# DeltaNet mixer: triangular inverse in eight pieces, pair assembly three tiles later, three gate tiles last

## The chip, the cores and the metric

One Trainium2 chip, one of its cores. The metric is the device time of one execution in microseconds (us), smaller is better. Shown times are medians of several runs.

## What is computed

A trunk of two layers over 512 frames of width 1024: an even layer (pooling and sparse attention), a gated DeltaNet layer, and a gated convolutional FFN after each. The change lies in the DeltaNet layer alone, whose core per head and per chunk of 64 frames is

```
proj = h @ w_in                                  # q, k, v (1024 each), gate 1024, beta 8, a 8
q, k, v = silu(causal_dwconv(qkv, conv_w))       # width 4
a     = einsum(k * beta, k) * dec_strict         # 64 x 64, strictly lower
t_mat = inverse of (a + eye)                     # triangular, unit diagonal
u, w  = t_mat @ (v * beta), t_mat @ (k * beta * exp(gc))
attn  = einsum(q, k) * dec_incl
# over the chunks:
v_new = u - w @ state;  o = q_dec @ state + attn @ v_new
state = state * decay + k_dec^T @ v_new
out   = rms_norm(o) * silu(gate) @ w_out
```

## The kernel before

Products with the large weights are made of three matmuls each (`mm3`, lines 101 to 106): weights and activations are split into a high and a low part. `split` (lines 94 to 99) makes the high part on ACT (L97) and the low part on DVE or POOL (L98, by a list). A projection tile is 128 output columns: 24 matmuls of 128x512 into one of four PSUM banks named `main`. Weights are loaded by SP (L110) three tiles ahead and split two tiles ahead.

`odd` builds the DeltaNet layer. Its loop goes over 32 projection tiles in `ORDER`: g (gate), k, q, v, each with a head number 0 to 7. After each tile it

- evacuates the tile: `gate` is one ACT instruction (L946) and a store to DRAM (L949); k, q and v tiles go through `conv`, one ACT instruction (L1020) and three of DVE (L1022), and later a SiLU on ACT (L1023);
- calls `pump`, which advances every running generator by one step. `k_chain`, `q_chain` and `v_chain` transpose and multiply a head some tiles later (L1038, L1067, L1093), and their results are read from PSUM by ACT (L1043) or DVE (L1095, L1082). POOL masks the result of L1095 (L1096). These small results use a ring of three PSUM banks named `chain`;
- writes PE's, ACT's and DVE's instructions in just this order (a manual schedule), so that each of these engines waits in order.

`invert` (lines 1100 to 1120) inverts the 32x32 diagonal blocks of all heads and chunks, on DVE alone: 31 rounds j of a product (L1114) and a subtraction (L1115), then a transposing copy (L1118), and two stores to DRAM, `x_d` (L1119) and `xt_d` (L1120). It is started at tile q3, where it only loads (L1106); a `yield` ends a piece, the next piece is issued at the next tile's `pump`. The pieces are rounds 0 to 9, 10 to 16, 17 to 23, 24 to 30, in tiles g5, q4, q5 and q6.

`y_chain` (lines 1125 to 1168) assembles the 128x128 inverses of two heads (a pair) out of these blocks. It is started four times, at the tiles in `YS`. Its steps, one a tile: load blocks from `x_d` (L1130, the first pair only) and `xt_d` (L1137) into a zeroed tile (L1132); nothing; multiply (L1143); multiply (L1150); transpose and multiply (L1158, L1160); multiply (L1167). What is not done after the last tile is done at once by `drain`. Then the recurrence over chunks of 128 frames begins: `step`, which uses the assembled inverse in L1253.

`QUIET` names the tiles whose low part is made on DVE; the other tiles' low parts of this layer are made on POOL.

Of the kernel before, what the change touches and what calls it, by code (L numbers as in the profile page):

```python
# [26 lines left out]
class Trunk:  # L27
# [89 lines left out]
    def load_rows(self, src, r0, tags=("wh", "wl"), lo_eng=None):  # L117
# [4 lines left out]

    FIRST = 5

    ORDER = [(t[0], int(t[1])) for t in ("g0 g1 g2 g3 g4 k0 k1 k2 k3 k4 k5 k6 k7 q0 q1 q2 q3 g5 "
                                         "q4 q5 q6 q7 v0 v1 v2 v3 v4 v5 v6 v7 g6 g7").split()]


    QUIET = [("q", 4), ("q", 5), ("q", 6), ("q", 7)]
    YS = [("v", 0), ("v", 2), ("v", 4), ("v", 6)]  # L130

    def tiles(self, kind):

# [2 lines left out]
        if kind == "o":  # L136
            col = {"g": 3 * D, "k": D, "q": 0, "v": 2 * D}
            return [(4 * D, 16)] + [(col[k] + n * P, P) for k, n in self.ORDER]
        return [(1152, P), (1280, P), (1408, 68), (1024, P)] + [(512 + j * P, P) for j in range(4)] + [(j * P, P) for j in (3, 2, 1, 0)]
# [760 lines left out]
    def odd(self, i, l, h):  # L900
# [5 lines left out]
        def k1(name, n=P):  # L906
            return self.s([P, n], name, bufs=1)
# [21 lines left out]
        beta, t1, t2, t3, g, gc = (k1(n, NH) for n in ("beta", "t1", "t2", "t3", "g", "gc"))  # L929
# [6 lines left out]
        v4 = lambda p: p.rearrange("p (t s) -> p t s", s=P)  # L936
# [89 lines left out]
        def silu():  # L1026

            for fn in late:
                inst = fn()
                self.after(inst, self.exp)  # L1030
                if self.hold is None:
                    self.hold = inst
            late.clear()
# [66 lines left out]
        def invert():  # L1100
            ad = a_d.rearrange("h t c s -> (h t) c s")
            As = self.b("xn", [P, 32, 32])
            Xs = self.b("xn", [P, 32, 32])
            for q in range(NB):
                r = slice(32 * q, 32 * q + 32)
                nc.sync.dma_start(As[r], ad[:, r, r])  # L1106
            nc.vector.memset(Xs, 0.0)
            nc.vector.memset(Xs.rearrange("p i j -> p (i j)")[:, ::33], 1.0)
            yield
            for j in range(31):  # L1110
                n, m = 31 - j, j + 1
                t = self.b("c", [P, 256])
                tv = t[:, :n * m].rearrange("p (i k) -> p i k", k=m)
                nc.vector.tensor_tensor(tv, As[:, j + 1:, j:j + 1].to_broadcast([P, n, m]), Xs[:, j:j + 1, :m].to_broadcast([P, n, m]), op=ALU.mult)  # L1114
                nc.vector.tensor_tensor(Xs[:, j + 1:, :m], Xs[:, j + 1:, :m], tv, op=ALU.subtract)  # L1115
                if j in (9, 16, 23):
                    yield
            nc.vector.tensor_copy(As, Xs.rearrange("p i j -> p j i"))  # L1118
            nc.sync.dma_start(x_d.rearrange("q b i j -> (q b) i j"), Xs)  # L1119
            nc.sync.dma_start(xt_d.rearrange("q b i j -> (q b) i j"), As)  # L1120
# [51 lines left out]
        nc.vector.tensor_copy(sel, self.ident[:H, :H].unsqueeze(2).to_broadcast([H, H, P]))  # L1172
        lo = [nc.gpsimd] * (len(self.ORDER) + 1)
        for kind, n in self.QUIET:
            lo[1 + self.ORDER.index((kind, n))] = nc.vector
        todo = []
        E = mybir.EngineType
        with self.tc.manual_schedule(engines={E.PE, E.Activation, E.DVE}):
            out = self.projs(win, self.tiles("o"), h, self.begin, lo)
            ba = self.b("c", [16, S])  # L1180
            nc.scalar.activation(ba, next(out), AF.Copy)
            for kind, hd in self.ORDER:
                p = next(out)
                if kind == "g":
                    silus.append(gate(hd, p))
                    if hd == 0:
                        todo = scalars(ba, silus[0])
                        next(todo)
                    elif hd == 4:
                        for _ in todo:  # L1190
                            pass
                        self.go(self.side(i))
                elif kind == "k":
                    conv(D + hd * P, p, kh(hd))
                    if hd < 3:
                        decays(range(3 * hd, min(H, 3 * hd + 3)))
                    self.go(k_chain(hd))
                elif kind == "q":
                    if hd % 2 == 0:
                        qT += pairs(1)  # L1200
                    conv(hd * P, p, qh(hd))
                    self.go(q_chain(hd))
                    if hd == 3:
                        self.go(invert())
                    if hd == 7:
                        nc.vector.scalar_tensor_tensor(c2, br2, -1.0, eg, op0=ALU.mult, op1=ALU.mult)
                else:
                    self.go(v_chain(hd, conv(2 * D + hd * P, p)))
                    if hd == 3:
                        nc.vector.tensor_scalar(fq, fq, P ** -0.5, None, op0=ALU.mult)  # L1210
                if (kind, hd) in self.YS:
                    self.go(y_chain(self.YS.index((kind, hd))))
                self.pump()
                if (kind, hd) not in self.ORDER[5:7]:
                    silu()
# [137 lines left out]
```

## Time and profile before

| | us |
|---|---|
| median of 3 runs (lowest, highest) | 1312.59 (1309.11, 1315.81) |
| the profiled execution, its own time | 1322.84 |
| its span, first to last instruction | 1320.8 |
| PE busy in the span | 1254.3 (95%) |
| DVE busy | 826.9 (63%) |
| ACT busy | 583.5 (44%) |
| POOL busy | 342.6 (26%) |

Times inside the span are counted from its first instruction. The DeltaNet projection tiles after q3 run from 742.7 to 866.6 us. Matmuls are pipelined, so the time of a row of PE is best read from one start to the next. Mean granted TensorE clock of the span: 0.969 of full speed.

### The profile page before, as it was taken

The page shows a single profiled execution, that of the slowest core. Times are in us where ns is not written, and L with a number is a line of the kernel's source. Part 1 is how long each engine was busy: PE and PEld are TensorE (multiplying, and loading weights), DVE is VectorE, ACT ScalarE, POOL GpSimd, SP SyncE. Part 2 cuts the span into 40 slices and gives each one's busy share as a digit, 9 for nine tenths or more (in the row PEclk, how much of TensorE's full clock was granted, in tenths as well). Part 3 has the DMA queues.
Part 4 walks back from the last instruction along what each step waited for, and adds up shares of the span by engine and source line. Part 5 has one row for each costly group of instructions (what it writes and reads, how often), then busy time and mean ns, then how long its engine had stood idle before and what let it go on. Part 6 is the DMA issues. An engine that isn't in the chain of part 4 may idle for free.

```text
span 1320.8 us, 17326 instructions
## 1 busy us (share of the span) xinstructions
PE 1254.3 (95%) x6359; PEld 1025.2 (78%) x6359; DVE 826.9 (63%) x1396; ACT 583.5 (44%) x1069; POOL 342.6 (26%) x294
## 2 busy tenths in 40 slices
PE   4998999899999999999999989999999999999997
PEld 3656565798888888888878868888798888888885
DVE  5599764457787678545256696436647765556328
ACT  3564656463433343326365424435655343334220
POOL 4477466350100010002356327200380010000001
PEclk9999598999999999999999999989899999999998
DMA  9952534326555538541236537473234633323221
GB/s 267 244 171 79 160 112 134 107 74 206 187 198 184 180 128 276 180 131 33 89 95 170 143 82 182 143 249 127 68 93 144 223 112 96 96 80 112 96 64 64
DMA packets 222474, 184.19 MB, mean 139 GB/s; under 512 B 24607, under 2 KB 191724, under 8 KB 222390
## 3 DMA queue, kind: packets, MB, share of 16 engines
q1 hardware_dynamic: 222390, 183.09, 45.8%
q8 instruction: 50, 0.82, 0.3%
q14 instruction: 34, 0.28, 0.1%
HBM read 169.29 MB, written 13.64 MB: 139 GB/s over the span
## 4 chain that ended last, share of the span: by engine, by line
PE 72%; DVE 12%; DMA 6%; ACT 4%; POOL 3%; issue 2%; SPq 1%; DVEq 0%; POOLq 0%; ACTq 0%
PE main L103 18%; PE main L104 18%; PE main L105 18%; PE chain L104 2%; PE chain L105 2%; PE chain L103 2%; DMA g<-in_e_mod_w_dram 1%; DVE wl L98 1%; PE side L103 1%; DVE g L716 1%; PE side L105 1%; PE side L104 1%; DVE m L715 1%; DMA mr<-in_f_mod_w_dram 1%; DVE xn L1115 1%
## 5 line engine op out<-in xcount | busy, mean ns | idle before, releaser
L103 PE MATMUL main<-h,wh 128*128 128x512 f32 (+2 forms) x1104 | 413.8, 379 | 3.6 <-ACT h L461 3.1
L104 PE MATMUL main<-h,wh 128*128 128x512 f32 (+2 forms) x1104 | 413.1, 375 | 2.7 <-DVE h L462 1.6
L105 PE MATMUL main<-h,wl 128*128 128x512 f32 (+2 forms) x1104 | 412.6, 374 | 2.3 <-DVE wl L98 1.7
L97 ACT ACTIVATE wh<-wr 128x1024 fp32r<-128x1024 f32 x176 | 184.0, 1049 | 280.6 <-PE main L104 192.9
L98 DVE TENSOR_TENSOR wl<-wr,wh 128x1024 fp32r<-128x1024 f32 x130 | 172.9, 1332 | 166.8 <-ACT wh L97 166.8
L103 PEld LDWEIGHTS main<-h,wh 128*128 128x128 f32 (+1 forms) x1104 | 207.4, 189 | 43.6 <-ACT h L461 4.1
L104 PEld LDWEIGHTS main<-h,wh 128*128 128x128 f32 (+1 forms) x1104 | 208.4, 189 | 41.2 <-DVE h L462 2.7
L105 PEld LDWEIGHTS main<-h,wl 128*128 128x128 f32 (+1 forms) x1104 | 208.1, 189 | 40.3 <-DVE wl L98 2.1
L98 POOL TENSOR_TENSOR wl<-wr,wh 128x1024 fp32r<-128x1024 f32 (+1 forms) x46 | 109.5, 2385 | 72.1 <-ACT wh L97 51.3
L542 DVE SCALAR_TENSOR_TENSOR t<-main,cw,t 128x511 f32<-128x511 f32 (+1 forms) x164 | 121.5, 744 | 2.0
L495 POOL TENSOR_TENSOR rstd<-rstd,mhalf 128x1 f32<-128x1 f32 x16 | 10.4, 651 | 395.1 <-DVE rstd L494 364.9
L1022 DVE SCALAR_TENSOR_TENSOR t<-main,ocw,t 128x511 f32<-128x511 f32 (+2 forms) x72 | 53.9, 748 | 57.5 <-ACT t L1020 55.8
L337 POOL TENSOR_TENSOR acc<-acc,mr 1x512 f32<-1x512 f32 x8 | 11.5, 1447 | 257.4 <-DVE acc L288 191.2
L282 POOL TENSOR_TENSOR acc<-acc,mr 128x512 f32<-128x512 f32 x42 | 55.2, 1321 | 33.7 <-ACT mr L280 30.7
L540 ACT ACTIVATE t<-main,cb,cw 128x512 f32<-128x512 f32 x82 | 62.2, 760 | 0.0
L547 ACT ACTIVATE t<-t 128x512 f32<-128x512 f32 x42 | 26.4, 628 | 59.5 <-DVE t L542 59.4
L103 PE MATMUL main<-wh,h 128*128 128x512 f32 x128 | 50.2, 392 | 0.0
L104 PE MATMUL main<-wl,h 128*128 128x512 f32 x128 | 50.0, 391 | 0.0
L105 PE MATMUL main<-wh,h 128*128 128x512 f32 x128 | 49.8, 390 | 0.0
L288 DVE SCALAR_TENSOR_TENSOR acc<-g,cs,acc 128x1024 f32<-128x1024 f32 x35 | 44.7, 1277 | 0.3
L280 ACT ACTIVATE mr<-mr,cs 128x512 f32<-128x512 f32 x42 | 30.1, 720 | 25.7 <-DMA mr<-in_f_mod_w_dram 12.9
L405 ACT ACTIVATE chain<-chain,B,G 128x128 f32<-128x128 f32 x84 | 33.2, 433 | 12.0 <-PE chain L397 11.4
(394 smaller groups left out, 2084.5 us busy)
## 6 DMA issues: line engine op xcount, KB each, us to landing
wr<-in_f_w_up_dram SPq DMA_DIRECT2D x84, 512.0 KB
wr<-in_f_w_down_dram SPq DMA_DIRECT2D x42, 512.0 KB
wr<-in_o_w_in_dram SPq DMA_DIRECT2D x32, 512.0 KB
g<-in_o_mod_w_dram SPq DMA_DIRECT2D x24, 512.0 KB
g<-in_e_mod_w_dram SPq DMA_DIRECT2D x32, 256.0 KB
mr<-in_f_mod_w_dram SPq DMA_DIRECT2D x32, 256.0 KB
g<-in_f_mod_w_dram SPq DMA_DIRECT2D x16, 512.0 KB
t<-in_f_mod_w_dram SPq DMA_DIRECT2D x32, 256.0 KB
```

The lines of the kernel that those rows point to most:

```text
L97: nc.scalar.activation(hi, src, AF.Copy)
L98: (lo_eng or nc.vector).tensor_tensor(lo, src, hi.bitcast(F32), op=ALU.subtract)
L103: inst = mm(ps, l[0], r[0], start=start, stop=False)
L104: mm(ps, l[0], r[1], start=False, stop=False)
L105: mm(ps, l[1], r[0], start=False, stop=stop)
L280: inst = nc.scalar.activation(r, raw, AF.Copy, scale=c)
L282: nc.gpsimd.tensor_tensor(part, part, r, op=ALU.add)
L288: nc.vector.scalar_tensor_tensor(part, raw, c, part, op0=ALU.mult, op1=ALU.add)
L405: nc.scalar.activation(t[:, c, :], t[:, c, :], AF.Identity, scale=G[:, k:k + 1], bias=B[:, k:k + 1])
L540: nc.scalar.activation(t, p, AF.Identity, bias=cb[:, n:n + 1], scale=cw[:, 4 * NF + n:4 * NF + n + 1])
L542: nc.vector.scalar_tensor_tensor(t[:, k:], p[:, :S - k], cw[:, 2 * NF * (2 - k) + n:2 * NF * (2 - k) + n + 1], t[:, k:], op0=ALU.mult, op1 ...
L1022: nc.vector.scalar_tensor_tensor(t[:, k:], p[:, :S - k], cw[:, 24 * (3 - k) + n:24 * (3 - k) + n + 1], t[:, k:], op0=ALU.mult, op1=ALU.add)
```

## The change

Three tables and one condition are altered. The gate tile g5 moves from between q3 and q4 to the end, so that the last three tiles are g5, g6, g7. `invert` yields after every fourth round, which makes eight pieces, in q4 to q7 and v0 to v3. `YS` moves the starts of the four pairs from v0, v2, v4, v6 to v3, v5, v7, g5. `QUIET` gains v0 to v3: their low parts go from POOL to DVE.

```
-    ORDER = [... "g0 g1 g2 g3 g4 k0 k1 k2 k3 k4 k5 k6 k7 q0 q1 q2 q3 g5 "
-                 "q4 q5 q6 q7 v0 v1 v2 v3 v4 v5 v6 v7 g6 g7").split()]
-    QUIET = [("q", 4), ("q", 5), ("q", 6), ("q", 7)]
-    YS = [("v", 0), ("v", 2), ("v", 4), ("v", 6)]
+    ORDER = [... "g0 g1 g2 g3 g4 k0 k1 k2 k3 k4 k5 k6 k7 q0 q1 q2 q3 q4 "
+                 "q5 q6 q7 v0 v1 v2 v3 v4 v5 v6 v7 g5 g6 g7").split()]
+    QUIET = [("q", 4), ("q", 5), ("q", 6), ("q", 7), ("v", 0), ("v", 1), ("v", 2), ("v", 3)]
+    YS = [("v", 3), ("v", 5), ("v", 7), ("g", 5)]
...
-                if j in (9, 16, 23):
+                if j % 4 == 3:
                     yield
```

How the instructions move is seen at three places. The first is SP's queue around the stores of the inverted blocks (`xn` is the blocks, `g` the tile of a pair, `wr` raw weights, `at_d` and `vb_d` results put aside for the recurrence). Before:

```order
L1119 DMA x_d<-xn_6387 128x1024
L1120 DMA xt_d<-xn_6386 128x1024
L1130 DMA xn_6812<-x_d 32x32x32 x4
L942 DMA at_d<-c_6740 128x4x128
L110 DMA wr_6906<-in_o_w_in_dram 128x8x128
L942 DMA at_d<-c_6797 128x4x128
L1137 DMA g_1258_6817<-xt_d 32x8x32 x4
```

Now:

```order
L1119 DMA x_d<-xn_6387 128x1024
L1120 DMA xt_d<-xn_6386 128x1024
L942 DMA vb_d<-c_6932 128x4x128
L110 DMA wr_7079<-in_o_w_in_dram 128x8x128
L1130 DMA xn_6935<-x_d 32x32x32 x4
L1137 DMA g_1277_6940<-xt_d 32x8x32 x4
```

The stores now end the piece in tile v3, and the loads of the first pair stand right behind them, in the same tile. Before, the stores ended the piece in q6, and the loads came in v0, two tiles later.

The second place is PE at the first matmuls on a pair's blocks (L1143). Before, they follow tile v2:

```order
L105 MATMUL main_6881<-h_834_4210,wl_6784 128x512
L1093 MATMUL chain_6917<-g_1231_6656,g_1031_5240 128x128 x4
L1038 MATMUL chain_6926<-ident,t_6787 128x128 x4
L1143 MATMUL chain_6934<-g_1258_6817,g_1036_5245 128x64 x8
L103 MATMUL main_6952<-h_831_4207,wh_6851 128x512
```

Now they follow tile v5:

```order
L105 MATMUL main_6992<-h_834_4210,wl_6906 128x512
L1038 MATMUL chain_7028<-ident,t_6909 128x128 x4
L1143 MATMUL chain_7036<-g_1277_6940,g_1036_5245 128x64 x8
L103 MATMUL main_7054<-h_831_4207,wh_6974 128x512
L104 MATMUL main_7054<-h_835_4211,wh_6974 128x512
```

From the piece that ends the inverse to L1143 there were four tiles (q7, v0, v1, v2), now there are two (v4, v5). From q3 to L1143 there were eight tiles (g5, q4 to q7, v0 to v2), now there are ten (q4 to q7, v0 to v5).

The third place is PE after the last projection tile, up to the first state update of the recurrence (L1260). Before:

```order
L105 MATMUL main_7408<-h_834_4210,wl_7285 128x512
L1167 MATMUL chain_7436<-c_7386,c_7385 64x64 x8
L1150 MATMUL chain_7446<-c_7398,xn_6812 32x32 x16
L1253 MATMUL main_7518<-h_1354_7499,g_1258_6817 128x128 x2
L1253 MATMUL main_7518<-h_1354_7499,g_1278_6945 128x128 x2
L1253 MATMUL main_7525<-h_1354_7499,g_1300_7094 128x128 x2
L1158 MATMUL chain_7466<-ident,g_1323_7252 64x64 x8
L1160 MATMUL chain_7467<-g_1323_7252,g_1039_5248 64x64 x8
L1167 MATMUL chain_7488<-c_7485,c_7484 64x64 x8
L1260 MATMUL main_7532<-c_7523,h_1355_7502 128x128 x4
```

Now:

```order
L1143 MATMUL chain_7403<-g_1327_7279,g_1039_5248 128x64 x8
L1253 MATMUL main_7518<-h_1354_7499,g_1277_6940 128x128 x2
L1253 MATMUL main_7518<-h_1354_7499,g_1294_7047 128x128 x2
L1158 MATMUL chain_7415<-ident,g_1318_7203 64x64 x8
L1160 MATMUL chain_7416<-g_1318_7203,g_1038_5247 64x64 x8
L1150 MATMUL chain_7437<-c_7412,xn_6935 32x32 x16
L1167 MATMUL chain_7456<-c_7434,c_7433 64x64 x8
L1158 MATMUL chain_7466<-ident,g_1327_7279 64x64 x8
L1160 MATMUL chain_7467<-g_1327_7279,g_1039_5248 64x64 x8
L1253 MATMUL main_7525<-h_1354_7499,g_1318_7203 128x128 x2
L1167 MATMUL chain_7488<-c_7485,c_7484 64x64 x8
L1260 MATMUL main_7532<-c_7523,h_1355_7502 128x128 x4
```

Ahead of these twelve rows stand L1167 and L1150, as before. One L1143, one L1150, one pair of L1158 and L1160 and one L1167 more than before lie behind the last tile; they lay between tiles before.

## Rows read from the trace of the kernel before

**Rows 1.** Timeline of PE after q3: start, duration, instruction, [idle before it, releaser].

```profile
742.70 0.48 PE L103 MATMUL main<-h,wh 128*128 128x512 f32 x1
...
749.51 0.48 PE L103 MATMUL main<-h,wh 128*128 128x512 f32 x1
...
762.70 0.48 PE L103 MATMUL main<-h,wh 128*128 128x512 f32 x1
...
768.59 0.48 PE L103 MATMUL main<-h,wh 128*128 128x512 f32 x1
...
770.99 0.50 PE L105 MATMUL main<-h,wl 128*128 128x512 f32 x1 [1.68 <-DVE wl L98]
...
788.60 1.11 PE L1038 MATMUL chain<-ident,g 128*128 128x128 f32 x4 [4.58 <-ACT junk L1043]
...
806.79 1.97 PE L1143 MATMUL chain<-g,g 128*128 128x64 f32 x16
```

**Rows 2.** A stretch: length, busy time of each engine, granted clock (PEclk), DMA share, GB/s.

```profile
788.60:794.60 6.00, 6.00 (x16) 4.87 (x17) 5.62 (x15) 0.00 (x0) 1.35 (x2) 0.50 0.74 249
```

**Rows 3.** Timeline of DVE, q3 to the end of the inverse.

```profile
742.37 2.32 DVE L1022 SCALAR_TENSOR_TENSOR t<-main,ocw,t 128x511 f32<-128x511 f32 x3 [1.62 <-ACT t L1020]
...
751.72 0.21 DVE L1114 TENSOR_TENSOR c<-xn,xn 128x31 f32<-128x31 f32 x1
...
758.50 1.22 DVE L98 TENSOR_TENSOR wl<-wr,wh 128x1024 fp32r<-128x1024 f32 x1
759.64 2.31 DVE L1022 SCALAR_TENSOR_TENSOR t<-main,ocw,t 128x511 f32<-128x511 f32 x3
761.86 0.68 DVE L1095 TENSOR_TENSOR c<-chain,g 128x512 f32<-128x512 f32 x1
...
762.95 1.39 DVE L1115 TENSOR_TENSOR xn<-xn,c 128x231 f32<-128x231 f32 x1
...
774.12 1.40 DVE L1115 TENSOR_TENSOR xn<-xn,c 128x252 f32<-128x252 f32 x1
775.56 2.47 DVE L1114 TENSOR_TENSOR c<-xn,xn 128x247 f32<-128x247 f32 x1
778.06 0.42 DVE L1115 TENSOR_TENSOR xn<-xn,c 128x247 f32<-128x247 f32 x1
...
786.61 2.48 DVE L1115 TENSOR_TENSOR xn<-xn,c 128x135 f32<-128x135 f32 x1
...
791.27 1.08 DVE L1118 COPY xn<-xn 128x1024 f32<-128x1024 f32 x1
```

**Rows 4.** Timeline of POOL in the same stretch.

```profile
762.62 1.46 POOL L1096 TENSOR_TENSOR c<-c,up 128x512 f32<-128x512 f32 x1 [9.91 <-DVE fq L1073]
...
775.21 2.54 POOL L98 TENSOR_TENSOR wl<-wr,wh 128x1024 fp32r<-128x1024 f32 x1
```

**Rows 5.** Timeline of SP: the issue of stores and loads (x4: four together).

```profile
738.93 0.36 SPq L1070 DMA_DIRECT2D a_d<-g  x1
741.73 2.41 SPq L1106 DMA_DIRECT2D xn<-a_d  x4
...
791.27 0.34 SPq L1119 DMA_DIRECT2D x_d<-xn  x1
...
794.62 2.20 SPq L1130 DMA_DIRECT2D xn<-x_d  x4
```

**Rows 6.** Timeline of PE after the last projection tile.

```profile
866.63 1.14 PE L1167 MATMUL chain<-c,c 64*64 64x64 f32 x16
...
868.72 1.87 PE L1253 MATMUL main<-h,g 128*128 128x128 f32 x12
870.52 0.63 PE L1158 MATMUL chain<-ident,g 64*64 64x64 f32 x8
...
872.90 1.87 PE L1167 MATMUL chain<-c,c 64*64 64x64 f32 x16 [0.68 <-ACT c L1163]
```

**Rows 7.** A stretch after the last tile, columns as in group 2.

```profile
878.00:880.00 2.00, 1.34 (x7) 1.04 (x5) 0.69 (x1) 0.63 (x2) 0.00 (x0) 0.53 0.16 66
```

More of the change, by code (lines that the diff above doesn't have):

```diff
@@ L123 @@
     FIRST = 5
-    ORDER = [(t[0], int(t[1])) for t in ("g0 g1 g2 g3 g4 k0 k1 k2 k3 k4 k5 k6 k7 q0 q1 q2 q3 g5 "
-                                         "q4 q5 q6 q7 v0 v1 v2 v3 v4 v5 v6 v7 g6 g7").split()]
-    QUIET = [("q", 4), ("q", 5), ("q", 6), ("q", 7)]
-    YS = [("v", 0), ("v", 2), ("v", 4), ("v", 6)]
+    ORDER = [(t[0], int(t[1])) for t in ("g0 g1 g2 g3 g4 k0 k1 k2 k3 k4 k5 k6 k7 q0 q1 q2 q3 q4 "
+                                         "q5 q6 q7 v0 v1 v2 v3 v4 v5 v6 v7 g5 g6 g7").split()]
+    QUIET = [("q", 4), ("q", 5), ("q", 6), ("q", 7), ("v", 0), ("v", 1), ("v", 2), ("v", 3)]
+    YS = [("v", 3), ("v", 5), ("v", 7), ("g", 5)]
     def tiles(self, kind):
```

## The prediction

> **What bounds the kernel now.** I first read the page for shares: PE is busy nearly all the time, so a change can win only where PE stands still or runs at half clock. Then the timeline of PE from q3 on, the only place that the change touches ahead of the last tiles. The reader should look at the starts there [rows 1]. A tile with its small multiplications (eight of L1093 and four transposes) takes 6.81 us from start to start (742.70 to 749.51), one with only the transposes 5.89 (762.70 to 768.59). PE's work from 742.70 to the first multiplication on a pair's blocks (L1143) would thus need 20.00 for three tiles (to 762.70), 5.89 for q6, and four times 6.81 for q7 and v0 to v2: it would be there at 795.83. It is there at 806.79. **10.96 us are lost**: 1.68 for the low part of weights that DVE makes late, 4.58 for a bank of the chain ring that ACT reads late, since ACT waits in order behind DVE [rows 1]; then 6.0 us at a granted clock of 0.50, which is 1.2 GHz [rows 2], half of which, 3.0, is lost; some 1.7 are scattered. That is 0.8% of the kernel, and all that spreading the inverse can win.
>
> The cause is DVE, whose timeline shows it without a pause from 751.72 on [rows 3]: the four pieces of the inverse stand in its order between the convolutions, the first 6.8 us long (751.72 to 758.50). The units of its work, start to start: the low part of a weight tile 1.14 (758.50 to 759.64), a convolution 2.22 (to 761.86), L1095 or L1082 0.68. From 751.72 to 791.27 are 39.55 us; two low parts, three convolutions and two L1095 take 10.30 of them. Of the 29.25 that are left, four instructions that normally take about 0.42 (as the one at 778.06) took 1.39, 1.40, 2.47 and 2.48: 6.06 too much. The inverse itself is thus 23.2 us.
>
> The timeline of POOL shows why those four were long [rows 3, 4]: POOL started the mask (L1096) at 762.62 and a low part (L98) at 775.21, and DVE's next instruction with two SBUF operands ended only when POOL had ended. So a mask beside the inverse costs 0.97, a low part on POOL beside it 2.05.
>
> **What the change removes.** The four pieces become eight, so that DVE has 23.2 us to place in eight tiles, about 2.9 in each. I count what DVE must do before the last piece ends in v3. It starts with the convolution of q4, one tile after that of q3: 742.37 + 6.81 = 749.18 [rows 1, 3]. Then come eight convolutions (17.76), five low parts (those of q7 and v0 to v3, 5.70), seven L1095 and one L1082 (5.44) and the inverse (23.2): 52.1, to 801.3. In q4, q5 and q6 the mask runs beside the piece, as at 762.62: 3 x 0.97 = 2.9. The low parts of v4 and v5 stay on POOL and start after the SiLU of v1 and v2, while their pieces run: 2 x 2.05 = 4.1. **The inverse ends at 808.3**, 17 us later than before, with DVE behind from q5 on.
>
> In q7 and v0 the mask meets a low part on DVE instead. No row shows such a meeting. It costs between 0 and 0.97 each, by the nearest rows; I take 0, since the 774.12 instruction, too, shows DVE held only for the rest of what POOL runs [rows 3], and DVE here starts about when POOL does. The Trainium skill (SBUF — State Buffer, section "SBUF: two separate sides") says that VectorE and GpSimd lock a shared port pair for a whole instruction, and that whoever starts first holds the other off. By it the two meetings are a race: lost by DVE, they would set the end 1.9 later. It also speaks against a part of this change, for a low part moved to DVE still locks the pair against POOL.
>
> **What the change adds.** The stores, then loads that wait for them, then L1143 now follow within two tiles, where there were four. The store to `x_d` was issued at 791.27 and the loads that need it at 794.62: 3.35 [rows 5]. Four loads take SP 2.20 to issue, and now eight stand in a row ahead of L1143 (L1130, L1137): 4.40. The last must land; its nearest row is a store of 256 KB, 738.93 to 741.73, so 2.80 [rows 5], and I keep 0 and 3.35 (the 512 KB store) as ends. The weights that SP loads between need POOL's low part of v6, which by the count above is done about when the store lands, and cost nothing. **L1143 can run at 808.3 + 3.35 + 4.40 + 2.80 = 818.9.** An estimate from the Trainium skill (DMA: Bandwidth & Descriptors, section "Anatomy of one DMA — SWDGE (gpsimd) path", about 2.0 us and the bytes at 436 GB/s) gives 2.1 for a load of 32 KB, which would put it 0.7 earlier.
>
> When is PE there? From 742.70, seven tiles with both small multiplications (q4 to q7, v0 to v2), 47.67, and three with transposes (v3 to v5), 17.67: 808.0. It waits on the way, at v3 and v4, for chain banks that DVE reads late, but those waits only take from the one at L1143. In all it stands for 818.9 - 808.0 = 10.9. L1143 is in order ahead of v6, so nothing else of PE can fill it; ACT stands behind it with L1145 and the SiLU of v5. After such a wait PE ran at half clock for 6.0 us [rows 2]; I take the same 3.0. **Lost now: 13.9, against 10.96: +2.9.**
>
> **The gates and the end.** Moving g5 changes no work: a gate needs one ACT instruction and one store, and DVE nothing, so the last three tiles leave DVE and ACT free for the pairs. But y2's last two steps and y3's last three now lie behind the last tile, one L1143, L1150, L1158 with L1160, and L1167 more than before. Their durations: 1.97 for L1143 [rows 1]; the others are what lies between 866.63 and 872.90 without the L1253 (868.72 to 870.52) and the 0.68 of waiting: 3.79 [rows 6]. These 5.8 us left earlier tiles, so at full clock they cost nothing. Their waits are covered: while ACT and DVE work for one pair, PE has the other's. Yet before, 6.3 us after the start of such work (872.90) L1167 took 1.87 where the one at 866.63 took 1.14, and the clock was still at half near 878 [rows 6, 7]. If the added work runs at half clock it costs its length again, 5.8. Between 0 and 5.8 I take 2, nearer the lower end, because in 872.2 to 872.9 PE also stood, and the new order leaves no such hole.
>
> **The sum: +2.9 + 2.0 = +4.9 us.** On the profiled execution's own 1322.84 that is 1327.7; that run lies 10.2 above the median of the runs shown, 1312.59, so the forecast is **1317.5**, no change that can be told: a measurement of this kernel tells about 0.5%, 6.6 us.
>
> **Rivals.**
>
> *Assembly behind the last tile at half clock: slower.* All the small multiplications after the first 6 us behind g7 run at 1.2 GHz. For it: so they did before [rows 6, 7]. Against it: the fall came together with a hole. Price 5.8 in place of 2: 2.9 + 5.8 = +8.7, 1321.3. It decides over the sign from 3.7 us on (2.9 + 3.7 = 6.6). Chance 0.37, with the upper bounds of the wait below.
>
> *The blocks come in time: faster.* If DVE were not behind, L1143 would find its blocks, and 8 to 10.96 of the loss would go: about 1303. For it: the early pieces fit a tile (q4: 2.22 + 0.68 + 1.14 + 2.9 = 6.94 against 6.81). Against: the stretches by POOL, and even with the inverse ended at 801.3, without one of them, L1143 could run only at 811.9, 3.9 late. Chance 0.12.
>
> **How the numbers follow.** The forecast has 0.51. Its own bounds: without the two 2.05 and with a landing of 0, L1143 runs at 812.0: idle 4.0, with 3.0 of clock 7.0, -4.0, and 0 at the end: 1308.6. With two masks (1.9), a third low part on POOL in v3 (2.05), a 3.35 landing (0.55) and another 3 us for a longer half clock: +2.9 + 7.5 = +10.4, and 5.8 at the end, 1328.8. The range for 8 in 10 leaves out the faster rival and the very top: 1307 to 1326. Slower by over 0.5% (1319.2) 0.37, within 0.5% 0.51, faster (below 1306.0) 0.12.
>
> **What would show it.** Right: in the changed profile PE waits some 8 us ahead of L1143 behind v5, put down to the `xt_d` load or to nothing known; the two old waits (L105 on DVE's L98, 1.68; L1038 on ACT, 4.58) are gone or under 2 each; the copy L1118 starts near 808; half clock follows the wait. Wrong: L1143 starts within 2 us of the end of v5's transposes, or the copy stands near 800; or PE waits for DVE's low parts in v0 to v3. The end is told by the time from L1167 after g7 to L1260, and the clock there.

## The result and the profile after

| | before | changed |
|---|---|---|
| median of 7 runs each | 1312.87 us | 1322.79 us |
| lowest to highest | 1309.11 to 1318.59 | 1319.27 to 1330.84 |
| profiled execution: own time / span | 1322.84 / 1320.8 us | 1321.04 / 1319.3 us |
| from the first L956 to the first L1241 | 637.0 to 881.9: 244.9 us | 624.3 to 881.1: **256.8 us** |
| from there to the end of the span | 438.9 us | 438.2 us |

The ratio is 1.0103, interval 1.0068 to 1.0139: the change makes the kernel **slower by 1%**, by 8.9 to 18.2 us. The forecast, 1317.5 and no change that can be told, was wrong, though 1322.79 lies in its range.

The two spans say nothing of this. The first L956, the head of the stage, stands at 637.0 in one execution and at 624.3 in the other, and all that is ahead of it is the same code. The clock differs there: from 100 to 200 us it was granted at 0.83 in the one and at 0.97 in the other. So I compare the stretch from L956 to the first L1241: **+11.9 us**. To set a start of the changed profile beside one of before, add 12.7 (637.0 - 624.3) to it.

Timeline of DVE, changed kernel, in the eight pieces of the inverse:

```profile
739.61 1.24 DVE L1115 TENSOR_TENSOR xn<-xn,c 128x31 f32<-128x31 f32 x1
...
766.46 1.22 DVE L98 TENSOR_TENSOR wl<-wr,wh 128x1024 fp32r<-128x1024 f32 x1
...
773.99 1.22 DVE L98 TENSOR_TENSOR wl<-wr,wh 128x1024 fp32r<-128x1024 f32 x1
...
779.47 2.46 DVE L1115 TENSOR_TENSOR xn<-xn,c 128x207 f32<-128x207 f32 x1
...
787.66 2.34 DVE L1114 TENSOR_TENSOR c<-xn,xn 128x112 f32<-128x112 f32 x1
...
795.26 1.13 DVE L1118 COPY xn<-xn 128x1024 f32<-128x1024 f32 x1
```

And of POOL:

```profile
766.61 2.23 POOL L1096 TENSOR_TENSOR c<-c,up 128x512 f32<-128x512 f32 x1 [5.78 <-issue]
...
774.08 2.28 POOL L1096 TENSOR_TENSOR c<-c,up 128x512 f32<-128x512 f32 x1 [4.27 <-DVE fq L1073]
...
779.13 2.57 POOL L98 TENSOR_TENSOR wl<-wr,wh 128x1024 fp32r<-128x1024 f32 x1 [0.90 <-ACT wh L97]
```

The inverse ends at 795.26, which is 807.96 on the clock of [rows 3]. Then SP takes over (its timeline, start and duration of each issue):

```profile
795.25 0.34 SPq L1119 DMA_DIRECT2D x_d<-xn  x1
796.42 0.34 SPq L1120 DMA_DIRECT2D xt_d<-xn  x1
797.01 0.37 SPq L942 DMA_DIRECT2D vb_d<-c  x1
798.65 0.38 SPq L110 DMA_DIRECT2D wr<-in_o_w_in_dram  x1
799.14 4.55 SPq L1130 DMA_DIRECT2D xn<-x_d  x4
803.74 2.42 SPq L1137 DMA_DIRECT2D g<-xt_d  x4
```

Against [rows 5] the four loads of L1130 took more than twice their 2.20. PE stood from the end of v5's transposes until the last of the loads of L1137 had landed (timeline of PE, multiplications of projection tiles left out, the first two rows at L1143, the others behind g7):

```profile
797.03 0.60 PE L1038 MATMUL chain<-ident,t 128*128 128x128 f32 x4
808.03 3.65 PE L1143 MATMUL chain<-g,g 128*128 128x64 f32 x16 [10.40 <-DMA g<-xt_d]
...
853.62 1.14 PE L1167 MATMUL chain<-c,c 64*64 64x64 f32 x16
...
855.72 2.35 PE L1143 MATMUL chain<-g,g 128*128 128x64 f32 x16
...
864.34 1.97 PE L1167 MATMUL chain<-c,c 64*64 64x64 f32 x16
...
877.54 2.07 PE L1260 MATMUL main<-c,h 128*128 128x128 f32 x8 [0.75 <-ACT c L1255]
...
881.11 1.06 PE L1241 MATMUL main<-acc,g 128*128 128x128 f32 x8
```

The old waits of [rows 1] (1.68 at L105, 4.58 at L1038) are gone; one of 1.5 at L1038 is left. In their place stands one of 10.40. The stretches of the same places (length, busy time of PE, PEld, DVE, ACT, POOL, granted clock, DMA share, GB/s):

```profile
808.00:814.00 6.00, 5.96 (x22) 5.51 (x23) 0.00 (x0) 2.06 (x3) 0.10 (x1) 0.50 0.67 159
...
854.00:856.00 2.00, 2.00 (x49) 1.89 (x46) 1.36 (x2) 1.57 (x3) 0.00 (x0) 1.00 0.97 300
856.00:858.00 2.00, 2.00 (x17) 2.00 (x17) 0.66 (x2) 0.00 (x0) 0.00 (x0) 0.80 1.04 277
858.00:879.00 21.00, 20.25 (x152) 18.63 (x152) 2.22 (x4) 6.64 (x17) 0.00 (x0) 0.50 0.55 191
```

So the 11.9 us have two places.

- **At L1143.** It starts at 820.73 on the clock of before. From L1143 to L1150 it took 11.33 (808.03 to 819.36), the first 8 us of it at 1.2 GHz; before it was 7.45 (806.79 to 814.24). Counted from 742.70 as in the prediction, 12.7 of waiting and standing and 3.9 of clock are lost, 16.6 in place of 10.96: **+5.6**.
- **Behind g7.** From the first L1167 behind it to the first L1241 are 27.49 us (853.62 to 881.11) in place of 15.28 (866.63 to 881.91). 5.8 of these 12.2 are the moved multiplications, whose time earlier tiles got back. **+6.4** are left. PE is busy 20.25 of the 21.00 us from 858 on, at a granted clock of 0.50, which is 1.2 GHz.

### The profile page after: what moved, and what is told of

Read it like the earlier page. It is cut to its first block, busy times and chain, and to the rows that moved or that the text cites. A ratio compares the mean times of both kernels' runs of the same rounds, so it can differ in the third digit from the quotient of the medians.

```text
span 1319.3 us, 17319 instructions
## 1 busy us (share of the span) xinstructions
PE 1251.5 (95%) x6359; PEld 1028.0 (78%) x6359; DVE 824.2 (62%) x1400; ACT 583.0 (44%) x1069; POOL 336.8 (26%) x290
## 4 chain that ended last, share of the span: by engine, by line
PE 73%; DVE 11%; DMA 6%; ACT 3%; issue 3%; POOL 2%; SPq 1%; DVEq 0%; ACTq 0%; POOLq 0%
PE main L103 18%; PE main L104 18%; PE main L105 18%; PE chain L104 2%; PE chain L105 2%; PE chain L103 2%; DVE t L1022 2%; DMA mr<-in_f_mod_w_dram 1%; DMA wr<-in_e_w_in_dram 1%; PE side L103 1%; PE side L104 1%; PE side L105 1%; DVE wl L98 1%; DMA g<-in_e_mod_w_dram 1%; POOL acc L282 1%
## 5 line engine op out<-in xcount | busy, mean ns | idle before, releaser
L105 PE MATMUL main<-h,wl 128*128 128x512 f32 (+2 forms) x1104 | 413.1, 375 | 0.0
L105 PEld LDWEIGHTS main<-h,wl 128*128 128x128 f32 (+1 forms) x1104 | 208.1, 189 | 37.3 <-issue 0.2
L98 POOL TENSOR_TENSOR wl<-wr,wh 128x1024 fp32r<-128x1024 f32 (+1 forms) x42 | 100.9, 2408 | 72.7 <-ACT wh L97 64.1
L495 POOL TENSOR_TENSOR rstd<-rstd,mhalf 128x1 f32<-128x1 f32 x16 | 10.4, 652 | 395.3 <-DVE rstd L494 364.8
L105 PE MATMUL main<-wh,h 128*128 128x512 f32 x128 | 49.8, 390 | 0.0
L409 DVE TENSOR_TENSOR h<-chain,h 128x256 fp32r<-128x256 f32 x48 | 19.5, 419 | 30.8 <-ACT h L408 30.3
```

What stands on the lines that cost most here:

```text
L98: (lo_eng or nc.vector).tensor_tensor(lo, src, hi.bitcast(F32), op=ALU.subtract)
L105: mm(ps, l[1], r[0], start=False, stop=stop)
```

## The experiments

The theory after the result: two losses, independent of each other, the wait at L1143 that the late inverse sets, and half clock behind g7. The rival: one of them carries it all, or the gate's place does. The ratios are to the kernel before, run on the same chips. Tail stands for the time from the first L1167 behind g7 to the first L1241.

| kernel | ratio, interval | L956 to L1241 | wait at L1143 | tail |
|---|---|---|---|---|
| before, two profiles | 1 | 244.9 / 243.3 | 0 / 0 | 15.28 / 13.74 |
| changed, two profiles | 1.0103, 1.0068 to 1.0139 | 256.8 / 255.5 | 10.4 / 10.6 | 27.49 / 27.45 |
| six pieces, two profiles | 1.0012, 0.9982 to 1.0042 | 234.9 / 246.5 | 0 / 0 | 17.35 / 27.49 |
| six pieces, pairs early | 1.0041, 1.0011 to 1.0071 | 245.0 | 7.9 | 12.17 (order of before) |
| `x_d` loads moved | 1.0082, 1.0051 to 1.0113 | 248.8 | 9.5 | 21.51 |
| low parts of v0 to v3 on POOL | 1.0124, 1.0065 to 1.0182 | 259.5 | 10.9 | 26.05 |
| more multiplications behind g7 | 1.0046, 1.0018 to 1.0074 | 252.9 | 10.4 | 24.97 |
| g5 alone moved | 1.0034, 1.0003 to 1.0064 | 243.2 | 0.5 | (two steps fewer) |
| six pieces, two pairs together, two profiles | **0.9954, 0.9924 to 0.9983** | 236.2 / 236.6 | 2.5 / 2.8 | (three steps fewer) |

**Six pieces in place of eight** (changed kernel, one line; `e1_six` in the expectations):

```diff
-                if j % 4 == 3:
+                if j % 6 == 5:
```

> The changed kernel with a yield after every sixth round (six pieces, the last one, round 30 alone, in v1 instead of v3); starts of the pairs as changed. My theory (the stores and loads between the end of the inverse and L1143 do not fit into two tiles): the inverse ends about 10 us earlier, the wait of 10.4 us ahead of L1143 falls to 0 to 3; PE waits 3 to 5 us for low parts or chain banks that DVE makes late in v0 to v3; the end behind g7 stays as long as now (27.5 us from L1167 to L1241). Against the changed kernel -9 to -13 us, so about as fast as the kernel before. Rival (DVE's load per tile decides, and longer pieces are worse): the old waits come back in full, and it is no faster than the changed kernel.

Measured: 1.0012, some 0.9% under the changed kernel. The copy L1118 stands 159.1 us behind L956 (630.5 to 789.6) where eight pieces put it at 171.0 (624.3 to 795.3), and L1143 finds its blocks. PE's waits on the way there, from q4 on, add up to 4.1, inside the 3 to 5 expected. The wait at L1143 was the late inverse's. But the profile also showed what I had not asked for: behind g7 the same instructions as in the changed kernel, at full clock throughout. Stretch and timeline of PE:

```profile
848.00:865.00 17.00, 16.15 (x222) 15.00 (x222) 4.52 (x8) 8.64 (x20) 0.00 (x0) 1.00 0.84 304
```

```profile
848.05 1.14 PE L1167 MATMUL chain<-c,c 64*64 64x64 f32 x16
...
850.15 2.00 PE L1143 MATMUL chain<-g,g 128*128 128x64 f32 x16
...
855.68 1.14 PE L1167 MATMUL chain<-c,c 64*64 64x64 f32 x16
...
865.40 1.06 PE L1241 MATMUL main<-acc,g 128*128 128x128 f32 x8
```

**Both kernels once more.** Is the half clock a matter of the kernel, or of the execution? The changed kernel and the one with six pieces were profiled again as they were.

> The changed kernel once more, for a second look at the same instructions. Theory (the half clock behind the last tile is a matter of the single execution, as e1_six with the very same instructions there ran at full clock): the wait ahead of L1143 is 10 to 10.8 us again, but the stretch from L1167 to L1241 lies anywhere between 17.4 and 27.5 us. Rival (the changed kernel always falls to half clock there, about 3.5 us behind the last tile): 27 to 28 us again.

> e1_six once more. Theory (chance of the execution): its 17.4 us from L1167 to L1241 were luck, which its times (1304 to 1321 us) suggest; this look shows between 17.4 and 27.5, and a span that is longer by as much. Rival (six pieces keep the clock up, since PE does not stand still for 10 us some 40 us earlier): 17.4 again.

The changed kernel: 27.45, at half clock again, as the rival said; that this very kernel can keep its clock there was not seen. The one with six pieces, as the theory said, did not repeat its 17.35: stretch and timeline of PE in its second profile:

```profile
858.00:884.00 26.00, 25.25 (x198) 23.59 (x195) 4.34 (x8) 7.06 (x18) 0.00 (x0) 0.54 0.55 189
```

```profile
856.40 1.14 PE L1167 MATMUL chain<-c,c 64*64 64x64 f32 x16
...
858.50 2.38 PE L1143 MATMUL chain<-g,g 128*128 128x64 f32 x16
...
867.16 1.97 PE L1167 MATMUL chain<-c,c 64*64 64x64 f32 x16
...
883.89 1.06 PE L1241 MATMUL main<-acc,g 128*128 128x128 f32 x8
```

The same program took 17.35 us in one execution and 27.49 in another. The instructions are the same and PE is busy in both, 16.15 of 17.00 us in the one and 25.25 of 26.00 in the other; what differs is the granted clock. The two executions ran on two chips, but the chip alone does not decide it: on the first one's chip two other kernels with this order fell (tails of 26.05 and 21.51). So this order of work behind the last tile can go at either clock; among the six profiles that hold it four fell to half clock at the L1143 (the last of them with the low parts on POOL, 26.05), one at the second L1160 (the one with the moved loads, 21.51), and one stayed at 1.00. At the same tail of 27.49 the six pieces still take 246.5 from L956 to L1241, where the changed kernel takes 256.8 and 255.5: that is what the wait at L1143 costs. The two losses are separate: this profile has the second without the first, and that of the six pieces with the pairs early (below) has the first without the second.

**More multiplications behind g7** (changed kernel; 30 multiplications of a constant of ones, in fives ahead of the steps of pairs 2 and 3; this adds work whose result is overwritten):

```diff
+        def dense(pr, p, n):
+            if pr > 1:
+                for _ in range(n):
+                    mm(p, self.ones, self.ones.unsqueeze(1).to_broadcast([P, 4, P]), start=True, stop=True)
```

> The changed kernel with 30 matmuls of 128x512 on a constant (their result is overwritten) put in fives ahead of the assembly's multiplications of pairs 2 and 3, behind the last projection tile: 30 x 0.227 = 6.8 us of PE at full clock, and nothing else changed. Theory (the clock falls there because the assembly's matmuls are small and thin, for lack of activity): PEclk stays at 1.00 there, and the stretch from L1167 after g7 to L1241, 27.5 us at half clock in the changed kernel and 17.4 in e1_six at full clock, takes 17.4 + 6.8 = 24.2, so -3 us although 6.8 us of work are added. Rival (the clock falls by chance or for the waiting on DMA and ACT, whatever PE does): PEclk falls as often, and the stretch takes 34 us or more in such a run: +7 us.

Measured: a tail of 24.97, shorter than 27.49 though PE does more. It is 7.62 above the 17.35 of the full clock, about what the added work takes there (7.98 from start to start; 6.8 was expected). Its stretch:

```profile
851.00:876.00 25.00, 24.25 (x253) 20.41 (x253) 4.63 (x8) 8.86 (x20) 0.00 (x0) 1.00 0.65 214
```

The ratio, 1.0046, is under the changed kernel's 1.0103, though the ends of the intervals overlap. One profile alone would not do, since the order can keep its clock by itself, but profile and ratio point the same way: what is lost behind g7 is clock. That wide multiplications between the small ones buy more of it than they cost in most executions is likely by the ratio, and not shown beyond this one profile.

**The low parts of v0 to v3 back on POOL** (changed kernel):

```diff
-    QUIET = [("q", 4), ("q", 5), ("q", 6), ("q", 7), ("v", 0), ("v", 1), ("v", 2), ("v", 3)]
+    QUIET = [("q", 4), ("q", 5), ("q", 6), ("q", 7)]
```

> The changed kernel with the old list: the low parts of v0 to v3 on POOL again. Theory (POOL's instructions hold off DVE's with two SBUF operands): DVE loses four low parts (4 x 1.14 = 4.6 us) but four more pieces meet a low part on POOL (4 x 2.05 = 8.2): the inverse ends 3 to 4 us later, and L1143 and the whole with it, +3 to +4 us. Rival (DVE's own work alone sets the end of the inverse): it ends 4.6 earlier, -4 to -5 us.

Measured: the copy L1118 174.8 us behind L956 (634.4 to 809.2), 3.8 later than 171.0. DVE saves four low parts of 1.14, 4.6 in all, and pays for it with four more stretched instructions. Two of the new ones, with POOL's beside them:

```profile
759.33 2.40 DVE L1115 TENSOR_TENSOR xn<-xn,c 128x175 f32<-128x175 f32 x1
...
775.93 2.55 DVE L1114 TENSOR_TENSOR c<-xn,xn 128x255 f32<-128x255 f32 x1
```

```profile
759.05 2.48 POOL L98 TENSOR_TENSOR wl<-wr,wh 128x1024 fp32r<-128x1024 f32 x1
...
775.79 2.40 POOL L98 TENSOR_TENSOR wl<-wr,wh 128x1024 fp32r<-128x1024 f32 x1 [2.82 <-ACT wh L97]
```

DVE's instruction ends, at 761.73 and 778.48, just after POOL's ends (761.53, 778.19). This part of the change, then, helps it, by the place of the copy; the ratio, 1.0124 from four runs, can't tell it from the changed kernel's.

**The `x_d` loads of the first pair behind the `xt_d` loads** (the block `if pr == 0` written behind the loop of L1137):

> The changed kernel with the four loads from xt_d (which L1143 needs) ahead of the four from x_d (which only L1150 needs). Theory (SP's issue in order is a part of the wait): the x_d loads took 4.55 us to issue, so L1143 starts 4 to 5.5 us earlier, its wait falls from 10.4 to about 5.5, the half clock after it stays: -4 to -5.5 us. Rival (the landing of the stores is what ends last): under 1.5 us.

Measured: a wait of 9.5, so that my 5.5 was wrong, and of the 8.0 us by which 248.8 is under 256.8 the tail makes up 6.0; but the run does not test what it was made for. SP has its own order:

```profile
800.48 0.38 SPq L110 DMA_DIRECT2D wr<-in_o_w_in_dram  x1
800.97 4.30 SPq L1137 DMA_DIRECT2D xn<-x_d  x3
805.37 2.08 SPq L1133 DMA_DIRECT2D g<-xt_d  x4
```

Three of the four `x_d` loads (128 KB each) still came first. They cost 4.30 right behind the load of 512 KB of weights, whose issue ended 0.11 ahead. In the changed kernel four cost 4.55 and 4.76, with 0.11 between, too, and 4.60 and 5.77 in its variants with more multiplications and with the low parts on POOL. Where the weights were issued over 5 us earlier, four cost 2.20 and 2.24 (before), 2.23 (six pieces, pairs early), 2.60 (g5 alone), 2.80 and 3.03 (six pieces), 2.93 and 3.10 (two pairs together). I take the weight load in front to be the cause; no run moved it alone, so that stays argued.

**Six pieces, and the pairs' steps from v1 on** (changed kernel with `j % 6 == 5` and `YS = [("v", 1), ("v", 3), ("v", 5), ("v", 7)]`):

> As e1_six, and the pairs start at v1, v3, v5, v7. The end of the inverse and L1143 are two tiles apart again, but everything is two tiles earlier, and what lies behind the last tile is what lay there in the kernel before. Theory: the wait ahead of L1143 is back (8 to 12 us, then half clock), and the stretch from L1167 after g7 to L1241 falls from 27.5 to about 15.3 us, 5.8 of it work that goes back to earlier tiles, so that the assembly behind the last tile costs 6.4: -5 to -8 against the changed kernel. Rival (the half clock behind g7 comes from something else than the added assembly work): the stretch at the end keeps more than half of its 6.4 us, and the time is within 3 of the changed kernel.

Measured: 1.0041. The wait is back with 7.9, and half clock behind it: L1143 took 3.65.

```profile
803.15 3.65 PE L1143 MATMUL chain<-g,g 128*128 128x64 f32 x16 [7.92 <-POOL wl L98]
```

The profile puts the end of this wait down to POOL's low part, which ended at 803.13, but L1143 does not read it. The last of its loads was issued by 801.40, 1.75 us ahead; in the changed kernel it was 1.87. So I take the loads to be what PE waited for. Six pieces, then, are not enough by themselves. With two tiles from the end of the inverse to L1143, as here, the wait is 7.9; with four (six pieces, pairs as changed) there was none. Behind g7 the order is that of the kernel before, and here it stayed at full clock: 12.17 from L1167 to L1241.

**The gate tile alone** (kernel before, only `ORDER` as in the change):

> The kernel before with the gate tile g5 moved behind v7 and nothing else. Every wait of the chunk-wise inverse now meets one tile less to hide behind, and the last pairs of assembly stand where they stood. Theory (the spreading of the inverse and the gate's place are separate: the gate brings the inverse's end and the wait at L1143 forward against the tiles, the end is lengthened by what stands behind g7, which is unchanged here): the stretch from L1167 behind g7 to the first L1241 stays near the kernel before's 15.28 us; the ratio to the kernel before lies between 0.997 and 1.005. Rival (the gate tile at the end is what costs): 1.005 to 1.011, the whole loss of the change.

Measured: 1.0034, inside the theory's 0.997 to 1.005, so the gate's place is not the whole loss; the upper end of its interval, 1.0064, leaves room for more than half. What I expected of the order was wrong: two steps (L1167 and L1150) fewer stand behind g7. In its profile the clock stayed at 1.00 there, and from L956 to L1241 it took 243.2, no longer than the kernel before; that it loses anything is shown by the ratio alone, and barely. What it pays appears ahead of L1143, for q4's tile no longer has the easy gate tile ahead of it (timeline of PE, rows that waited):

```profile
775.50 0.66 PE L1038 MATMUL chain<-ident,g 128*128 128x128 f32 x4 [2.48 <-ACT junk L1043]
786.76 2.07 PE L1093 MATMUL chain<-g,g 128*128 128x128 f32 x8 [5.13 <-ACT junk L1043]
791.12 1.12 PE L1038 MATMUL chain<-ident,g 128*128 128x128 f32 x4 [2.29 <-DVE c L1095]
```

These are 9.9 us where [rows 1] has 6.26. I take it that with the inverse in four long pieces the gate tile, which asks nothing of DVE, was a rest for it; no run tests this alone.

**The kernel before, once more.**

> The kernel before, unchanged, for a second profile. Theory (the half clock behind g7 is a chance of the execution that any of these kernels can meet): the stretch from L1167 behind g7 to the first L1241 takes 15.28 us again within 0.3 us, or differs from it with the granted clock of 868 to 881 us. Rival (only the changed order meets it): 15.28 within 0.3 us at the same granted clocks.

Its tail took 13.74 against 15.28, at other granted clocks (0.86 in the last 11.9 us, 0.71 in those of the first profile), as the theory had it. With the 12.17 of the same order above, the end before costs 1.6 to 3.1 us of clock. It, too, depends on the execution, but by 3 us, not by 10.

**Six pieces, and two pairs at a time** (changed kernel):

```diff
-    YS = [("v", 3), ("v", 5), ("v", 7), ("g", 5)]
+    YS = [("v", 2), ("v", 3), ("v", 6), ("v", 7)]
...
-                if j % 4 == 3:
+                if j % 6 == 5:
```

> Six pieces as in e1_six, pairs started at v2, v3, v6, v7: L1143 three tiles behind the end of the inverse, and less assembly behind the last tile (one L1143 and one L1167 less than changed). Theory: the wait ahead of L1143 is 0 to 3 us, the stretch behind the last tile is 2 to 6 us shorter than in e1_six in the mean of executions, so 2 to 6 us under e1_six's and 4 to 8 under the times of the kernel before: ratio 0.994 to 0.997. Rival (three tiles do not suffice either, or the chain ring now blocks with two pairs in step): a wait of 5 us or more in v4 to v7, no faster than the kernel before.

Measured: 1307.83 us, a ratio of 0.9954, interval 0.9924 to 0.9983: **faster than both kernels.** Row of the waits of PE (us in total, times, longest), then two stretches of its profile, at L1143 and behind g7:

```profile
PE chain L1143 <- DMA g<-xt_d: 2.5, 1, 2.5
```

```profile
796.70:802.70 6.00, 5.94 (x34) 5.26 (x35) 2.84 (x4) 3.19 (x5) 3.26 (x2) 1.00 0.98 241
848.00:862.00 14.00, 13.15 (x164) 11.81 (x163) 4.13 (x6) 7.41 (x18) 0.00 (x0) 1.00 0.84 326
```

With three tiles from the end of the inverse to L1143 the wait is short, and no half clock follows it. Behind g7 stand five small steps (L1158 with L1160 taken as one) in place of eight, and they run at 1.00. A second profile:

> The kernel with six pieces and the pairs assembled two and two, once more, for a second profile. Theory (the short stretch behind the last tile is the chance of the execution, but there are fewer instructions behind it than in the changed kernel, so that it is worth less): the stretch from L1158 of the last pair to the first L1241 takes 13.5 us at a granted clock of 1.00, or, in an execution at 0.50, 17 to 21 us. Rival (this order keeps the clock): 13.5 within 0.3 us.

From the first L1158 behind g7 to L1241 it took 13.48 us, after 13.47, both times at full clock, as the rival said. Two profiles don't show that it can't fall; the ratio of 12 runs holds what it did on average.

## Why the prediction was wrong

**The bound and the place** were right: behind the stretch from L956 to L1241 the two kernels take the same (438.9 and 438.2), and ahead of it their code is the same.

**The end of the inverse** was right: 808.3 was predicted, 807.96 came. So were its terms: masks that stretch the first subtraction (L1115) of three pieces to 1.24 to 1.36, low parts on POOL that stretch one instruction in v1 and one in v2 to 2.46 and 2.34. The two meetings of a mask with a low part on DVE took nothing from DVE, as I chose: DVE started first, at 766.46 and 773.99, and took its 1.22; POOL's masks started 0.15 and 0.09 later and took 2.23 and 2.28, where the mask of [rows 4] took 1.46. By the rule that I cited from the Trainium skill (SBUF — State Buffer, section "SBUF: two separate sides") these meetings are a race, and the trace agrees in these two: DVE started first, and POOL was held off.

**The wait at L1143** was right in kind and too small: +2.9 was predicted, +5.6 measured. The chain from the first store to L1143 was to take 10.55 (3.35 + 4.40 + 2.80) and took 12.78 (795.25 to 808.03). From the store's issue to the first load's it was 3.89; the eight loads took 7.02 to issue, of which the first four 4.55; the landing took 1.87. The term that was mis-sized is "Four loads take SP 2.20 to issue": that was read where no weights were issued just ahead. I had written of the weights between stores and loads that they "cost nothing"; that they are the cause is argued, the 4.55 is measured. The clock behind the wait took 3.9, not 3.0. The prediction's other estimate of the landing, 2.1, goes by a figure for the SWDGE (gpsimd) path, as it says itself; these loads are issued by SP, so that the 1.87 does not test it.

**The end** is the step that failed most: "Between 0 and 5.8 I take 2, nearer the lower end, because in 872.2 to 872.9 PE also stood, and the new order leaves no such hole." Measured: +6.4, above the upper end. The fall of the clock needed no hole: it came between 856 and 858, with PE busy 2.00 of 2.00 us there and in the two before. Nor did a hole bring it: the six pieces with the pairs early stood for the same 0.68 ahead of the last L1167 and stayed at full clock. And the bound of 5.8, the added work at half clock, left out that a longer stretch of small multiplications also takes along the ones that were there before: L1253, L1260, L1268 up to 881. At full clock the whole tail is 17.35; the changed kernel lost 10.1 there, where the kernel before lost 1.6 to 3.1 against the 12.17 of its own order. The two full-clock tails differ by 5.2, the 5.8 of moved work less the 0.68 of standing that the new order does without: there the prediction was right, and the clock is what was mis-sized. The rival "Assembly behind the last tile at half clock" named the right mechanism, and its price was too low for the same reason.

**The sum.** +5.6 and +6.4 make 12.0, where the sections differ by 11.9 and the ratio gives 8.9 to 18.2. The rival "The blocks come in time" did not come true here, but with six pieces it did (no wait at L1143), since DVE then ends 10.4 to 11.9 us earlier behind L956 (two profiles). Why five cuts end the inverse so much sooner than seven was not taken apart further: fewer meetings with POOL and fewer tiles' convolutions ahead of the last piece are both in it.

What stays open: why one execution keeps its clock behind g7 and another of the same program doesn't. The Trainium skill (TensorE: Matmul & The Clock Gate, section "What's actually happening") says that the number of slow multiplications with which one kernel starts differs from run to run. The two profiles of the six pieces differ from run to run, too, by 10.1 us, but in the middle of a kernel; whether that has the same cause no run here shows.

## What to carry to other kernels

Work that is spread to fill an engine's gaps also ends later: ask who waits for its end, and how many tiles lie between, ahead of asking which waits it removes. When the bound engine's small multiplications are moved to behind its last wide ones, price the whole run of them at half clock, the old ones too. And time such an end in more than one execution, for its profile may show either clock.

## What was not expected of the hardware

- The same program's tail took 17.35 us at a granted clock of 1.00 and 27.49 at 0.54, with PE busy for about 95% and 97% of the stretches shown.
- PE busy 20.25 of 21.00 us stayed at 1.2 GHz to the end of that stretch; with 30 wide multiplications put between, the longer run of work stayed at 1.00 in the one profile taken, and ended earlier (24.97).
- Four loads of 128 KB issued right behind a load of 512 KB took SP 4.55 to 5.77 us in four profiles, and 2.20 to 3.10 in eight where that load was issued over 5 us earlier.
